# Values centred where they are stored, and a readout with its sums on VectorE and a scaling on ScalarE

## The chip, the cores and the metric

The kernel runs on one core of a Trainium2 chip. TensorE (PE in the profile) multiplies matrices, VectorE (DVE), ScalarE (ACT) and GpSimd (POOL) work elementwise, and SyncE (SP) issues most transfers. The metric is the device time of one execution in microseconds, as the median of three runs. All data are float32; a product of two float32 matrices is made of three passes over high and low halves (H and L in the names).

## The reference

Two layers over 256 context tokens and 2048 latent tokens, 1024 wide: an RWKV mixer with 16 heads of 64, and a differential attention. The change touches the mixer's scan and its readout.

```python
def step(S, inp):
    r_t, w_t, k_t, v_t, kk_t, a_t = inp
    sa = jnp.einsum("bhvk,bhk->bhv", S, kk_t)
    S = (S * w_t[:, :, None, :]
         - sa[..., None] * (kk_t * a_t)[:, :, None, :]
         + v_t[..., None] * k_t[:, :, None, :])
    return S, jnp.einsum("bhvk,bhk->bhv", S, r_t)
...
mean = jnp.mean(o, axis=-1, keepdims=True)
var = jnp.mean(jnp.square(o - mean), axis=-1, keepdims=True)
y = ((o - mean) * lax.rsqrt(var + GN_EPS)).reshape(B, T, RW_WIDTH) * gn_g + gn_b
bonus = jnp.sum(jnp.sum(r[:, :, None] * kd * r_k, axis=-1, keepdims=True) * v[:, :, None], axis=2)
y = (y + bonus.reshape(B, T, RW_WIDTH)) * jax.nn.silu(g)
return y.astype(out_dtype) @ w_out
```

The scan starts from a state of zero and is linear in v, and each of the 64 rows of a head's state depends on its own element of v alone. So the mean of o over a head's 64 values is what the scan gives for the mean of v over them, and if v is centred per head and token, o comes out centred. The bonus uses v itself.

## The kernel before, in words

The program has stages, one after another: the first projection and the streams of the scan (to about 1150 us), the scan (to about 2250 us), the readout (to about 2600 us), the second projection, attention and its output projection.

**First projection.** Three groups of tokens, and in each eight pairs of heads. For every pair PE projects its columns (`project`, L363), and DVE and ACT make the streams of the scan from them. `by_token` turns the pair's values by PE's transposes, ACT copies them into the tile `vtok` (128 partitions, 6 blocks of tokens x 2 x 2 x 64), and after every second pair two transfers on SP store them (`S["v"]`, L550). So `vtok` is full 12 times. The gate of the pair is made by ACT and by two products on DVE (`sg`, L574). The weights of the next pair are cast on ACT, and their low half is a subtraction on DVE (`wL` and `w2L`, L92). The order of each engine is set by a scheduler here.

**Readout.** There are 18 tiles of 128 tokens. A tile needs: the sum of the two directions of the scan (`of`+`ob`, L972); its mean, the subtraction and the square (L977 to L980); the variance (L983, L984); the inverse root, an integer seed (L70) and three Newton steps of three instructions on a tile `st` of 17 columns (L72, L73, L79), 16 for the heads and one for the norm below; the product with it (`ob`, L988); eight transposes on PE (L995) and two products with the gate (L996); the sum with the bonus (`sgg`+`bv`, L998); and its halves `yH` (ACT, L91) and `yL` (DVE, L92). `product` multiplies them with the output weights, 48 matmuls (L932) in four quarters. `sums` multiplies a half of the result by a gate on DVE (`gated`, L1021) and adds it to x on POOL (L1022). `norms` squares and sums x on ACT (L1029), scales the sum (L1030), multiplies x by the inverse root (L1032), transposes it on PE (L214), which ACT brings into `ht` (L220), and stores `ht` for the second projection. Seven transfers of 512 KB belong to a tile: of, ob, sgg, bv and x in, x and ht out.

These are generators: each `yield` ends a step of a tile. The string `READ` says in which order the steps are issued in one round, and `in_order` makes each engine keep this order. A is the next step of the rows of the tile two ahead, B of the tile one ahead, M0 to M3 are the four quarters of this tile's product, G is `sums` of its first half, H `sums` of the second half of the tile before, N is a step of `norms` of the tile before, R a Newton step. One root instruction serves the 16 variances of the tile two ahead and the norm of the tile before. The pools hold two tiles each of `of`, `ob`, `sgg`, `bv`, `yH`, `yL` and `ht`, and three of x. Before the first round the first two tiles are worked ahead, in between the casts of the output weights (`split`).

## Time and profile before

| what | value |
|---|---|
| median of 3 runs | 5019.62 us (5014.31 to 5025.64) |
| profiled execution | 5014.9 us, its span 5013.2 us |
| PE busy | 4677.5 us (93%) |
| DVE busy | 3764.6 us (75%) |
| ACT busy | 2678.0 us (53%) |
| POOL busy | 1510.5 us (30%) |
| mean granted PE clock | 0.967 |
| readout, 2285 to 2597 us | PE 248.96 us busy, DVE 264.44 us |

A busy share is an average over stages. The span is what the profiler recorded; the profiled execution took 1.7 us longer. PE's clock has two levels, 2.4 GHz (1.00 in the profile) and 1.2 GHz (0.50). Lines such as L932 are those of the code above; a helper's line (L70 to L79, L91, L92, L214, L220) serves several stages, and the names of the tiles tell them apart.

### The profile page before, as it was taken

How to read it: one execution, taken by the hardware profiler on the slowest of the kernel's cores; microseconds unless marked ns; L12 is line 12 of the kernel's file. 1: busy time of each engine (PE TensorE's matmuls, PEld its weight loads, DVE VectorE, ACT ScalarE, POOL GpSimd, SP SyncE). 2: the span in 40 equal slices, each digit the busy share in tenths (PEclk: the TensorE clock that was granted, in tenths of full speed). 3: DMA queues.
4: the chain of work that ended last, by engine and by line, in shares of the span. 5: the costliest groups of instructions: out<-in, count | busy, mean ns of one | idle time of the engine just before them, and what ended most of it. 6: DMA issues, size and time to landing. Idle time of an engine off the chain costs nothing.

```text
span 5013.2 us, 101038 instructions
## 1 busy us (share of the span) xinstructions
PE 4677.5 (93%) x40786; PEld 4202.4 (84%) x40786; DVE 3764.6 (75%) x5833; ACT 2678.0 (53%) x4890; POOL 1510.5 (30%) x1840
## 2 busy tenths in 40 slices
PE   6999999997988989897879999999999999999999
PEld 5999999995888888875668888878888888898887
DVE  6778777777777778758878348328989989988843
ACT  4555555554666666653342122117777777777730
POOL 1121112113665566633322022022233323323300
PEclk8999999998999999988889999999999999999999
DMA  4565566557677666676653233240111011010042
GB/s 165 165 185 165 165 184 176 164 157 208 154 172 170 167 160 170 169 228 212 202 183 106 94 125 98 88 119 1 28 45 36 11 45 36 27 28 18 9 156 93
DMA packets 624787, 612.13 MB, mean 122 GB/s; under 512 B 31622, under 2 KB 529721, under 8 KB 623297
## 3 DMA queue, kind: packets, MB, share of 16 engines
q1 hardware_dynamic: 621841, 601.99, 41.6%
q8 instruction: 323, 5.29, 0.5%
q10 hardware_dynamic: 2480, 3.67, 0.3%
q14 instruction: 143, 1.17, 0.1%
HBM read 405.79 MB, written 199.77 MB: 121 GB/s over the span
## 4 chain that ended last, share of the span: by engine, by line
PE 36%; DVE 6%; issue 5%; ACT 2%; POOL 1%; DMA 0%; POOLq 0%; ACTq 0%; DVEq 0%; SPq 0%
PE mmps L932 16%; PE pv L1451 8%; PE tps L1444 4%; PE sc L1405 3%; PE sc L1406 3%; DVE p L1408 3%; DVE p L1429 2%; PE tps L1354 1%; DVE r L1426 1%; ACT at L1446 1%; ACT p L1419 1%; POOL out L1279 0%; PE tps L1594 0%; ACT ht L220 0%; ACT qt L1385 0%
## 5 line engine op out<-in xcount | busy, mean ns | idle before, releaser
L1419 ACT ACTIVATE p<-p,m 128x2304 f32<-128x2304 f32 x256 | 568.8, 2222 | 201.0 <-DVE p L1408 198.4
L1451 PE MATMUL pv<-v,at 128*128 128x128 f32 x4608 | 626.4, 277 | 6.3 <-ACT at L1446 4.4
L1451 PEld LDWEIGHTS pv<-v,at 128*128 128x128 f32 x4608 | 564.4, 192 | 16.2 <-ACT at L1446 12.9
L1405 PE MATMUL sc<-ks,qh 128*128 128x512 f32 (+1 forms) x1280 | 520.6, 407 | 15.3 <-DVE p L1408 15.2
L1406 PE MATMUL sc<-ks,ql 128*128 128x512 f32 (+1 forms) x1280 | 464.0, 372 | 0.3 <-POOL ql L1386 0.3
L363 PE MATMUL mmps<-hH,wH 128*128 128x386 f32 x1632 | 432.1, 345 | 18.6 <-DVE sg L574 12.3
L1446 ACT COPY at<-tps 128x512 f32<-128x512 f32 (+1 forms) x640 | 345.2, 540 | 179.4 <-PE tps L1444 175.5
L1429 DVE SCALAR_TENSOR_TENSOR p<-p,r,p 128x1152 f32<-128x1152 f32 x256 | 426.9, 1668 | 4.5
L363 PE MATMUL mmps<-hL,wH 128*128 128x386 f32 x1632 | 427.8, 342 | 2.1 <-DVE hL L92 2.1
L363 PE MATMUL mmps<-hH,wL 128*128 128x386 f32 x1632 | 426.7, 342 | 1.4 <-DVE nm_ss L197 1.2
L932 PE MATMUL mmps<-wH,hH 128*128 128x512 f32 x1088 | 424.8, 390 | 3.1 <-ACT hH L91 3.1
L932 PE MATMUL mmps<-wL,hH 128*128 128x512 f32 x1088 | 424.5, 390 | 0.0
L932 PE MATMUL mmps<-wH,hL 128*128 128x512 f32 x1088 | 424.0, 390 | 0.0
L1408 DVE TENSOR_SCALAR_CACHE_REDUCE p<-sc,m 128x1280 f32<-128x1280 f32 x256 | 395.5, 1545 | 18.1 <-PE sc L1406 1.6
L1386 POOL TENSOR_TENSOR ql<-qt,qh 128x256 fp32r<-128x256 f32 x128 | 113.5, 887 | 979.8 <-ACT qt L1385 918.5
L1444 PE MATMUL tps<-ident,p 128*128 128x128 f32 x2304 | 361.6, 275 | 10.3 <-ACT qt L1385 5.4
L1408 DVE TENSOR_SCALAR_CACHE_REDUCE p<-sc 128x1024 f32<-128x1024 f32 x256 | 311.5, 1217 | 56.7 <-PE sc L1406 55.6
L1444 PEld LDWEIGHTS tps<-ident,p 128*128 128x128 f32 x2304 | 273.2, 141 | 60.8 <-ACT at L1446 11.2
L363 PEld LDWEIGHTS mmps<-hH,wH 128*128 128x128 f32 x1632 | 298.4, 191 | 24.8 <-DVE sg L574 15.8
L363 PEld LDWEIGHTS mmps<-hL,wH 128*128 128x128 f32 x1632 | 301.4, 191 | 3.3 <-DVE hL L92 3.3
L363 PEld LDWEIGHTS mmps<-hH,wL 128*128 128x128 f32 x1632 | 302.0, 191 | 2.5 <-DVE nm_ss L197 2.0
L700 POOL TENSOR_TENSOR N<-N,rank 128x30 f32<-128x30 f32 (+14 forms) x510 | 278.8, 547 | 40.0
(315 smaller groups left out, 10779.0 us busy)
## 6 DMA issues: line engine op xcount, KB each, us to landing
wr<-in_rw_in_dram SPq DMA_DIRECT2D x102, 512.0 KB
s_qr<-QR SPq DMA_DIRECT2D x48, 768.0 KB
BK<-s_bk SPq DMA_DIRECT2D x72, 512.0 KB
s_bk<-BK SPq DMA_DIRECT2D x47, 768.0 KB
wraw<-in_da_in_dram SPq DMA_DIRECT2D x64, 512.0 KB
BA<-s_bk SPq DMA_DIRECT2D x72, 256.0 KB
LA<-s_qr SPq DMA_DIRECT2D x72, 256.0 KB
BB<-s_bk SPq DMA_DIRECT2D x72, 256.0 KB
```

Of the source, the lines that this page charges most:

```text
L363: nc.tensor.matmul(a[:, :b1 - b0], wt[:, kt, :], ht[:, kt, b0:b1], start=(kt == 0 and wt is wH and ht is hH), stop=(kt == KT - 1 and last))
L700: eng.tensor_tensor(N[:, m + 1:32, 0:m], N[:, m + 1:32, 0:m], t, op=ALU.subtract)
L932: k.nc.tensor.matmul(ps, s(kt), m(kt), start=(kt == 0 and s is sH and m is mH), stop=(kt == KT - 1 and last))
L1386: nc.gpsimd.tensor_tensor(ql, qt, qh.bitcast(F32), op=ALU.subtract)
L1405: nc.tensor.matmul(s[:, b0 - g0:b1 - g0], qh[:, cs], ks, start=True, stop=False)
L1406: nc.tensor.matmul(s[:, b0 - g0:b1 - g0], ql[:, cs], ks, start=False, stop=True)
L1408: nc.vector.tensor_scalar(tiles[n][c][:, g0:g1], s[:, :g1 - g0], -1.0, m, op0=ALU.mult, op1=ALU.min, accum_out=least)
L1419: nc.scalar.activation(P, P, AF.Exp, bias=m, scale=-1.0, accum_out=z)
L1429: nc.vector.scalar_tensor_tensor(P0[:, b0:b1], P1[:, b0:b1], r, P0[:, b0:b1], op0=ALU.mult, op1=ALU.add)
L1444: nc.tensor.transpose(ps[:, c - b0:c - b0 + 128], P0[:, c:c + 128], k.ident)
L1446: (eng.copy if eng is nc.scalar else eng.tensor_copy)(at[b][:, :b1 - b0], ps[:, :b1 - b0])
L1451: nc.tensor.matmul(acc, at[b][:, c - b0:c - b0 + 128], H.v[:, c // 128], start=(c == 0), stop=(c == T - 128))
```

## The change

It has two parts. In the first projection, when `vtok` is full, DVE sums each of its 24 groups of 64 values and subtracts a 64th of the sum from them; the store of v then takes the centred values. `vm`, from which the bonus is made, stays as it is.

In the readout the mean, its scaling and the subtraction are left out. The scalings of the variance and of the norm's sum go into the squares on ACT (by 1/8 and 1/32 before squaring), and both small constants are added by one instruction on 17 columns. The sums `of`+`ob` and `sgg`+`bv` of all tiles go to DVE, as the first tile's were before. The scaling of x by the inverse root goes from DVE to ACT. The loads of a tile become a step of their own (L, for the tile three ahead), `yL` becomes a step of its own behind `yH`, and `READ` is rewritten.

```diff
@@ -535,6 +535,8 @@
                 out = nc.scalar if end else nc.sync
 
                 def by_token(vtok):
                     if p % 2 == 0:
                         vtok = up.tile([128, 6, 2, 2, 64], F32, name="vtok", bufs=1)
                     for b in range(2):
@@ -545,6 +547,11 @@
                         nc.scalar.copy(vtok[:, 3 * b:3 * b + 3, :, p % 2, :],
                                        ps[:, :384].rearrange("p (j a v) -> p j a v", a=2, v=64))
                     if p % 2 == 1:
+                        heads = vtok.rearrange("p j a q v -> p (j a q) v")
+                        total = up.tile([128, 24], F32, name="vsum")
+                        nc.vector.tensor_reduce(total, heads, axis=AX.X, op=ALU.add)
+                        nc.vector.scalar_tensor_tensor(heads, bcast(total, 2, 64), -1.0 / 64, heads,
+                                                       op0=ALU.mult, op1=ALU.add)
                         for a in range(2):
                             c0 = a * 512 + (p - 1) * 64
                             nc.sync.dma_start(out=S["v"][gs, c0:c0 + 128].rearrange("(j p) c -> p j c", p=128),
@@ -933,7 +940,7 @@
                                stop=(kt == KT - 1 and last))
 
 
-READ = "B A A H M0 M1 A G N B R R M2 R N A M3 B N N"
+READ = "H A M0 B B N A B M1 R R R B G A N L M2 N N M3"
 
 
 def readout(k):
@@ -958,7 +965,11 @@
         gates = k.gates
         wH, wL = ([wps[half].tile([128, KT, 512], F32R, name=name) for half in range(2)] for name in ("woH", "woL"))
 
-        def rows(i, first):
+        eps = small.tile([128, 17], F32, name="eps", bufs=1)
+        nc.vector.memset(eps[:, :16], 64e-5)
+        nc.vector.memset(eps[:, 16:], 1e-6)
+
+        def rows(i):
 
 
 
@@ -969,19 +980,13 @@
             bv = gp.tile([128, NPAIR, 128], F32, name="bv")
             nc.sync.dma_start(out=flat(of), in_=S["o"][0, ts])
             nc.sync.dma_start(out=flat(ob), in_=S["o"][1, ts])
-            (nc.vector if first else nc.gpsimd).tensor_tensor(of, of, ob, op=ALU.add)
             nc.sync.dma_start(out=sgg, in_=S["sgg"][:, :, ts])
             nc.sync.dma_start(out=bv, in_=S["bv"][:, :, ts])
             yield
-            mean = small.tile([128, 16], F32, name="mean")
-            nc.vector.tensor_reduce(mean, of, axis=AX.X, op=ALU.add)
-            nc.vector.tensor_scalar(mean, mean, 1.0 / 64, None, op0=ALU.mult)
-            nc.vector.tensor_tensor(of, of, bcast(mean, 2, 64), op=ALU.subtract)
-            nc.scalar.activation(ob, of, AF.Square)
-            yield
-            var = stat.s[:, :16]
-            nc.vector.tensor_reduce(var, ob, axis=AX.X, op=ALU.add)
-            nc.vector.tensor_scalar(var, var, 1.0 / 64, 64e-5, op0=ALU.mult, op1=ALU.add)
+            nc.vector.tensor_tensor(of, of, ob, op=ALU.add)
+            nc.scalar.activation(ob, of, AF.Square, scale=1.0 / 8)
+            yield
+            nc.vector.tensor_reduce(stat.s[:, :16], ob, axis=AX.X, op=ALU.add)
             yield
             rstd = stat.y[:, :16]
             yn = flat(ob).rearrange("p (b c) -> p b c", c=128)
@@ -995,10 +1000,12 @@
                     nc.tensor.transpose(ps[:, 128 * j:128 * j + 128], yn[:, 4 * half + j], k.ident)
                 nc.vector.tensor_tensor(sgg[:, hs], ps.rearrange("p (a b) -> p a b", b=128), sgg[:, hs], op=ALU.mult)
                 yield
-            (nc.vector if first else nc.gpsimd).tensor_tensor(sgg, sgg, bv, op=ALU.add)
+            nc.vector.tensor_tensor(sgg, sgg, bv, op=ALU.add)
             yH = yp.tile([128, NPAIR, 128], F32R, name="yH")
             yL = yp.tile([128, NPAIR, 128], F32R, name="yL")
-            split_evac(k, yH, yL, sgg)
+            nc.scalar.copy(yH, sgg)
+            yield
+            nc.vector.tensor_tensor(yL, sgg, yH.bitcast(F32), op=ALU.subtract)
             yield yH, yL
 
         def product(i, yH, yL):
@@ -1025,11 +1032,9 @@
 
             def norms():
                 h = hp.tile([128, KT, 128], F32, name="ht")
-                ss = stat.s[:, 16:17]
-                nc.scalar.activation(flat(h), x, AF.Square, accum_out=ss)
-                nc.vector.tensor_scalar(ss, ss, 1.0 / D, 1e-6, op0=ALU.mult, op1=ALU.add)
+                nc.scalar.activation(flat(h), x, AF.Square, scale=1.0 / 32, accum_out=stat.s[:, 16:17])
                 yield
-                nc.vector.tensor_scalar(x, x, stat.y[:, 16:17], None, op0=ALU.mult)
+                nc.scalar.activation(x, x, AF.Copy, scale=stat.y[:, 16:17])
                 yield
                 for half in range(2):
                     flip_half(k, 1, which, tpb, x, h, 0, half)
@@ -1040,7 +1045,7 @@
 
         N = T // 128
         order = (1, 0, *range(2, N))
-        todo = [rows(i, j == 0) for j, i in enumerate(order)]
+        todo = [rows(i) for i in order]
 
         raws = {}
 
@@ -1067,6 +1072,8 @@
 
         def roots(c0, c1):
 
+            s = stat.s[:, c0:c1]
+            nc.vector.tensor_tensor(s, s, eps[:, c0:c1], op=ALU.add)
             for stat.y in rsqrt_steps(k, small, stat.s, 17, "st", c0=c0, c1=c1):
                 yield
 
@@ -1089,8 +1096,9 @@
                         load_gate(k, 0, which, gates[which])
             split(0)
             split(1)
-            for _ in range(3):
+            for _ in range(4):
                 y = step(todo[0])
+            step(todo[2])
             split(2)
             split(3)
         none = iter(())
@@ -1099,6 +1107,7 @@
             for j in range(N + 1):
                 nxt = todo[j + 1] if j + 1 < N else none
                 after = todo[j + 2] if j + 2 < N else none
+                far = todo[j + 3] if j + 3 < N else none
                 stat.s = small.tile([128, 17], F32, name="stat")
                 root = roots(0 if j + 2 < N else 16, 17 if j else 16)
                 if j < N:
@@ -1110,6 +1119,8 @@
                     kind = what[0]
                     if kind == "A":
                         step(after)
+                    elif kind == "L":
+                        step(far)
                     elif kind == "B" and j + 1 < N:
                         y = step(nxt)
                     elif kind == "M":
```

How the change moves instructions is seen at three places. In a step of the readout on DVE, before: from the scaling of x to the norm's sum, between two blocks of roots (`st`, 10 instructions that are left out here).

```order
L1032 TENSOR_SCALAR x<-x,st_y 128x1024
L988 TENSOR_TENSOR ob<-of,st_y 128x2x8x64
L92 TENSOR_TENSOR yL<-sgg,yH 128x1024
L996 TENSOR_TENSOR sgg<-tps,sgg 128x512
L977 TENSOR_REDUCE mean<-of 128x16
L978 TENSOR_SCALAR mean<-mean 128x16
L979 TENSOR_TENSOR of<-of,mean 128x1024
L1021 TENSOR_TENSOR gated<-mmps,gate_27254 128x512
L983 TENSOR_REDUCE stat<-ob 128x16
L984 TENSOR_SCALAR stat<-stat 128x16
L1021 TENSOR_TENSOR gated<-mmps,gate_27254 128x512
L1030 TENSOR_SCALAR stat<-stat 128x1
```

And after, at the same place (the roots stand before the first row and behind the last):

```order
L1008 TENSOR_TENSOR yL<-sgg,yH 128x1024
L1028 TENSOR_TENSOR gated<-mmps,gate_27290 128x512
L993 TENSOR_TENSOR ob<-of,st_y 128x2x8x64
L1028 TENSOR_TENSOR gated<-mmps,gate_27290 128x512
L986 TENSOR_TENSOR of<-of,ob 128x1024
L1001 TENSOR_TENSOR sgg<-tps,sgg 128x512 x2
L989 TENSOR_REDUCE stat<-ob 128x16
L1003 TENSOR_TENSOR sgg<-sgg,bv 128x1024
L1076 TENSOR_TENSOR stat<-stat,eps 128x17
```

Between two blocks of roots stand the two sums and one reduction; both products with the gate (`sgg`<-`tps`) stand together behind `of`+`ob`, and no scaling of x is left on DVE.

On ACT, one step of the readout before and the start of the next:

```order
L91 CAST yH<-sgg 128x1024
L220 ACTIVATE ht<-tps,mod_127 128x128 x8
L980 ACTIVATE ob<-of 128x1024
L1029 ACTIVATE ht,stat<-x 128x1024
L91 CAST yH<-sgg 128x1024
```

And after:

```order
L1037 ACTIVATE x<-x,st_y 128x1024
L220 ACTIVATE ht<-tps,mod_127 128x128 x8
L987 ACTIVATE ob<-of 128x1024
L1035 ACTIVATE ht,stat<-x 128x1024
L1006 CAST yH<-sgg 128x1024
```

The scaling of x stands between yH and the eight copies into `ht`, whose transposes read it.

On DVE in the first projection, the piece of the difference around the first new pair of instructions (`wr` and `w2r` are raw weights, `sg` is the gate):

```order
 L92 TENSOR_TENSOR wL<-wr,wH 128x1024
-L574 SCALAR_TENSOR_TENSOR sg<-sg,mmps 128x386 x2
+L581 SCALAR_TENSOR_TENSOR sg<-sg,mmps 128x386 x2
+L552 TENSOR_REDUCE vsum<-vtok 128x24
+L553 SCALAR_TENSOR_TENSOR vtok<-vsum,vtok 128x1536
 L92 TENSOR_TENSOR w2L<-w2r,w2H 128x512
 L402 TENSOR_TENSOR uk<-uk,km 128x768
```

The pair stands behind the gate's products and ahead of the low half of the weights; in some of the 12 places another instruction stands between the two.

## Rows read from the trace of the kernel before

**Rows 1.** Stages (us): busy time and instructions per engine, PEclk, DMA share, GB/s.

```profile
20.00:1160.00 1140.00, 1084.71 (x6191) 1046.92 (x6188) 875.11 (x1368) 641.39 (x1077) 223.54 (x180) 0.97 0.57 170
...
2222.00:2285.00 63.00, 45.97 (x541) 35.57 (x540) 41.18 (x63) 28.29 (x41) 7.67 (x4) 0.78 0.87 289
2285.00:2597.00 312.00, 248.96 (x1072) 206.13 (x1072) 264.44 (x391) 105.08 (x200) 118.17 (x66) 0.87 0.59 186
```

**Rows 2.** PE's waits, 2285 to 2600 us: total, times, longest.

```profile
PE tps L214 <- DVE x L1032: 57.1, 17, 5.4
```

**Rows 3.** The tile yL: duration min/median/max in ns, first and last start.

```profile
L92 DVE TENSOR_TENSOR yL<-sgg,yH x18: 1216/1219/1224, 2268.8 to 2583.1; 128x1024 fp32r<-128x1024 f32 x18
```

**Rows 4.** Timeline of one step of the readout: start, duration in us, engine, line.

```profile
2426.73 0.60 PE L995 MATMUL tps<-ident,ob 128*128 128x128 f32 x4
...
2427.78 0.68 DVE L996 TENSOR_TENSOR sgg<-tps,sgg 128x512 f32<-128x512 f32 x1
...
2429.09 2.39 POOL L998 TENSOR_TENSOR sgg<-sgg,bv 128x1024 f32<-128x1024 f32 x1
2429.20 2.32 DVE L72 TENSOR_TENSOR st_t<-st_y 128x17 f32<-128x17 f32 x1
...
2431.55 0.18 DVE L73 SCALAR_TENSOR_TENSOR st_t<-st_t,stat 128x17 f32<-128x17 f32 x1
2431.77 0.18 DVE L79 SCALAR_TENSOR_TENSOR st_y<-st_t,st_y 128x17 f32<-128x17 f32 x1
...
2432.29 2.35 POOL L972 TENSOR_TENSOR of<-of,ob 128x1024 f32<-128x1024 f32 x1 [0.81 <-issue]
2432.41 2.27 DVE L79 SCALAR_TENSOR_TENSOR st_y<-st_t,st_y 128x17 f32<-128x17 f32 x1
2432.44 0.39 PE L932 MATMUL mmps<-woH,yL 128*128 128x512 f32 x1
...
2436.07 1.22 DVE L988 TENSOR_TENSOR ob<-of,st_y 128x1024 f32<-128x1024 f32 x1
2436.30 1.94 PE L214 MATMUL tps<-ident,x 128*128 128x128 f32 x8 [3.47 <-DVE x L1032]
2437.21 1.22 DVE L92 TENSOR_TENSOR yL<-sgg,yH 128x1024 fp32r<-128x1024 f32 x1
```

**Rows 5.** Groups of 2285 to 2585 us: times run, busy us, mean ns, idle before.

```profile
L72 DVE TENSOR_TENSOR st_t<-st_y 128x17 f32<-128x17 f32 x45 | 42.1, 936 | 1.6
L1022 POOL TENSOR_TENSOR x<-x,gated 128x512 f32<-128x512 f32 x32 | 41.4, 1294 | 173.9 <-DVE gated L1021 120.2 <-issue 21.9 <-DMA wraw<-in_da_in_dram 13.3
...
L979 DVE TENSOR_TENSOR of<-of,mean 128x1024 f32<-128x1024 f32 x15 | 18.4, 1225 | 0.5
...
L977 DVE TENSOR_REDUCE mean<-of 128x16 f32<-128x1024 f32 x15 | 18.1, 1209 | 0.0
...
L1029 ACT ACTIVATE ht<-x 128x1024 f32<-128x1024 f32 x16 | 17.0, 1060 | 14.3 <-POOL x L1022 13.4 <-DMA x<-in_x_dram 0.9
...
L1032 DVE TENSOR_SCALAR x<-x,st_y 128x1024 f32<-128x1024 f32 x16 | 12.1, 753 | 1.9 <-DVE st_y L79 0.4
```

**Rows 6.** Slices of 1 us: PE busy (x), PEclk, DMA share, GB/s.

```profile
2439.00:2440.00 1.00, 1.00 (x4) 0.50 0.91 373
...
2441.00:2442.00 1.00, 1.00 (x4) 0.52 0.81 203
```

**Rows 7.** The chain of waits in the last stage: start, us, what.

```profile
4877.11 0.44 PE tps L1594 x4
4877.55 10.94 PE mmps L932 x48
```

**Rows 8.** Timeline of DVE before the first round of the readout.

```profile
2234.41 1.22 DVE L972 TENSOR_TENSOR of<-of,ob 128x1024 f32<-128x1024 f32 x1 [1.95 <-DMA ob<-s_o]
```

**Rows 9.** Timeline of PE at the end of the readout.

```profile
2597.55 1.09 PE L214 MATMUL tps<-ident,x 128*128 128x128 f32 x8 [2.20 <-DVE x L1032]
```

**Rows 10.** PE's waits in the first projection, 20 to 1160 us.

```profile
PE mmps L363 <- DVE sg L574: 12.3, 11, 2.3
```

## The prediction

> **What bounds the kernel now.** The table by stages comes first [rows 1]. In the first projection (20 to 1160 us) TensorE (PE) is busy for 1084.71 of 1140 us at a granted clock of 0.97: little to gain there. The readout (2285 to 2597 us) is the weak stage: PE 248.96 of 312 us, VectorE (DVE) 264.44, a clock of 0.87. The table of PE's waits names one cause: the transposes of x (L214) wait for DVE's scaling of x (L1032), 57.1 us in 17 times [rows 2]. A step is measured by yL, which DVE writes once a tile: 18 times from 2268.8 to 2583.1 us, 17 intervals, 314.3/17 = 18.49 us each [rows 3].
>
> Why the scaling is late stands in one step [rows 4]. POOL starts sgg+bv (L998) at 2429.09 for 2.39 us; beside it a DVE instruction of 17 elements takes 2.32 us, where its neighbours take 0.18. At 2432.29 POOL starts of+ob (L972) for 2.35 us, and again a small one takes 2.27. So each POOL sum costs DVE some 2.1 us, in the middle of the roots that the scaling needs. The groups say that this is the rule: 45 root instructions of one kind average 936 ns [rows 5]. PE's last matmul ends at 2432.83, and its transposes start at 2436.30 after 3.47 us idle. The second loss follows: the granted clock is at 0.50 (1.2 instead of 2.4 GHz) when they run, for 1.94 us, and comes back only in 2441 to 2442 [rows 6].
>
> **What PE needs.** At the full clock 48 matmuls take 10.94 us, 0.228 each, and 4 transposes 0.44 [rows 7]. A step has 48 matmuls (four quarters M0 to M3 of 2.73 us) and 16 transposes (two groups of 0.87 us): 10.94+1.74 = 12.7 us. That is the floor of a step.
>
> **The change, readout.** Per tile it takes the mean (1.21) and the subtraction (1.225) off DVE, three scalings of 16 or fewer columns (I price them as the small instructions, 0.18 [rows 4]), and the scaling of x, 0.75 [rows 5]: 3.7 us. It adds of+ob and sgg+bv, and one sum of 17 elements. On DVE the sum of+ob of the first tile took 1.22 [rows 8], and sgg+bv has the same shape. So DVE pays 2.4 and is rid of two stalls of 2.1: 4.2 us. Large sums with nothing to wait for start 1.14 us apart (2436.07, 2437.21), that is 0.08 less than their length; for 512 elements (0.68) that gives 0.60; dependent small ones start 0.21 apart (I take 0.213) [rows 4].
>
> The step in the new order, from the start of M0:
> - M0 ends at 2.73. Four transposes of ob (0.60 in a row at full clock, against 0.44 in the middle of a run [rows 7]; I take 0.60) and 0.05 to DVE: 3.38.
> - DVE multiplies two halves of sgg, 1.20: 4.58. Then the variance's reduction 1.14 and sgg+bv 1.14: 6.86. The reduction needs ScalarE's (ACT) square of of+ob, which starts when DVE's sum is done, about 2.1, and takes 1.06 [rows 5].
> - 11 small instructions (the sum with eps, the seed and 9 of three root steps) by 0.213: 9.20.
> - x is scaled on ACT. No row has this form with 1024 elements; between DVE's 0.75 and ACT's square of 1024 elements, 1.06 [rows 5], I take 1.06 (its own engine) and 0.05 on either side: 10.36.
> - Eight transposes 0.87: 11.23. M3 2.73: **14.0 us**.
> PE has M1 and M2 between its two groups of transposes and ends them at 2.73+0.87+5.46 = 9.06, so it waits 1.3 us, for ACT instead of DVE. What is late next is this one wait. DVE goes on with yL, one gated product and ob until about 12.7, hence ahead of the next M0; yH and yL are done 3 us before they are needed. POOL keeps the two sums of x (1.29 each [rows 5]); one may stall DVE's of+ob by up to 1.3 us, from 0.8 to 2.1, and DVE has nothing then before 3.38, so up to 0.3 us of it is felt. All loads of a tile stand one tile earlier and in another order on SP; the load of ob can go when the transposes of the tile before last have read its buffer, 3.6 us into a step, and is needed by of+ob 0.8 us into the next, 11 us later. 7 transfers of 512 KB per step are 3.67 MB in 14 us, 262 GB/s; one slice shows 373 [rows 6].
>
> Does the clock stay up with a wait of 1.3 us? After a wait of 2.20 us in the last tile the 8 transposes took 1.09 us, near the full clock's 0.87; after 3.47 us they took 1.94 [rows 4, 9]. I take the full clock.
>
> Gain: 17 x (18.49-14.0) = 76 us. Before the first yL (2268.84) two tiles' means, scalings and subtractions leave the chain, 2 x 2.6 us [rows 5]: 5 us (0 to 10; ACT's order around it changes too). Two steps also cast the next weights on ACT and DVE, two casts of 1024 elements each, as yL 1.2 us on DVE [rows 3]: 4 us of the gain is not had. The first steps run beside the stage's densest transfers (289 GB/s [rows 1]): another 4.
>
> **The change, first projection.** After every second pair of heads DVE gets a reduction of 1536 elements and a product-and-sum over them, 12 times. The nearest rows are the reduction and the subtraction of 1024 elements, 1.21 and 1.225 [rows 5]; by length 1.75 to 1.8 each, 3.5 a pair, 42 us on DVE, which is idle for 265 of 1140 us [rows 1]. They stand behind the gate's two products (L574) and before the weights' low half (L92 w2L) and uk. PE waited for DVE's gate products 12.3 us in 11 times, its most costly wait in this stretch [rows 10]; the new pair stands behind these products, and what comes after it (the next low halves, uk) PE needs later. The store of v now waits for DVE, and behind it on SP stand loads of weights used about a head later. I take 2 us, with 0 and 42 as ends. A gain is excluded: nothing is removed here. At the end of the stage the store of v delays the scan's first loads: 2 us (0 to 4). The rest of the program is as it was; the last tile adds 0.5 us for a scaling on ACT.
>
> **Sum.** -76-5+4+4+2+2+0.5 = -68.5 us. The profiled execution took 5014.9 us (span 5013.2, 1.7 around it); so 4946 for it. The median of the runs is 5019.6, 4.7 above: **4951 us**.
>
> **Rivals.**
> - *The clock falls in every step, as now.* A wait of 1.3 us then costs as much clock as 3.47 does now: from 2436.3 to 2441.9, 5.6 us at half, 2.6 us a step. Step 16.6, gain 17 x 1.9 = 32: 4995 us; with every second step about 4973. For: the stage now shows 0.87; against: [rows 9]. 0.17.
> - *PE alone sets the step.* If the roots end 1.3 us sooner than I reckon, the step is 12.7, 17 x 5.8 = 98: 4929 us. 0.08.
> - *DVE stays the bound.* It is busy for 264.44 of 312 us and gets 2.4 us of sums per step. If its stalls of 4.2 us stayed in the chain in another shape (POOL's sums of x, late loads of ob), x would be scaled at 14.6 and the step be 18.2: 17 x 0.3 = 5 us of gain there, 5022 us. Against: only sums of 1024 elements on POOL stand beside the long small instructions [rows 4], and these go. 0.03. The Trainium skill, "Perfetto Trace Analysis", section "Optimizing Scalar/DVE Operations", speaks for this rival: from a saturated VectorE work may be handed to ScalarE or even GpSimd, and the change hands two sums the other way. The same section adds that these two share an SBUF read port, so that offloading between them might not help; with that the rows agree, a stall of 2.1 us against 1.2 us for doing the sum oneself.
> - *Transfers set the step.* 3.67 MB at the stage's 186 GB/s [rows 1] are 19.7 us, so no gain: 5015 to 5025 us. The 373 GB/s of one slice speak against it [rows 6]. 0.02.
> - *Slower: the centring lands on PE's path.* Its pair of 3.5 us stands before w2L, uk and BK on DVE, and if PE waits for them it loses 3.5, a spell at half clock as in the readout (2.6), and some of the delay of the weights' loads that stand on SP behind the late store (up to 3.5 more; I take 1): 7.1 a pair, 12 of them 85 us against 2 in the sum, 5034 us. It decides from 5.9 us a pair (70.5/12). For: PE is busy for 95% of this stage, so nothing there hides a wait. Against: DVE idles for 22 us per pair (265/12). 0.05.
> That the change does not do what it says is excluded by its code: no sum of sgg or of is left on POOL.
>
> **Chances and range.** The forecast 0.65, with 4935 to 4972 from the ends above (a step of 13.5 to 14.8, startup, phase 1 up to 12). The two ends of the range take in the floor and most of the first rival: 4929 to 4988. Faster by over 0.2% (10 us, about what a measurement can tell): 0.65+0.17+0.08 = 0.90; within (the two rivals of no gain): 0.05; slower: 0.05.
>
> **What would show it.** Right: yL at intervals near 14.0; small DVE instructions in the roots at 0.18 throughout; PE's wait at the transposes of x (L214) 1 to 2 us and named after ACT; a clock near 1.00 from the second step on; first projection within 5 us of its length. Wrong: a wait above 2 us there with transposes of 1.9 us (the clock), a wait of DVE's of+ob for its loads (transfers), a longer first projection with PE waiting for w2L or hL (the centring).

## The result and the profile after

The changed kernel takes 4959.27 us (median of 4 runs, 4953.41 to 4979.01) against 5018.75 (4 runs, 5014.31 to 5025.64): ratio 0.9885, 95% interval 0.9861 to 0.9909. On another chip, later, it took 4959.15 (6 runs) against 5028.34 (12 runs): 0.9869 (0.9843 to 0.9895). The prediction was 4951, 4929 to 4988. It holds, and is 8 us low.

The tile yL measures the step, as in [rows 3]: a step is the time from one of its starts to the next.

```profile
L1008 DVE TENSOR_TENSOR yL<-sgg,yH x18: 1217/1218/1226, 2276.0 to 2518.1; 128x1024 fp32r<-128x1024 f32 x18
```

242.1 us for 17 intervals, 14.24 each, against 18.49. From the fourth to the fifteenth all are 14.2 (14.17 on average); the first three are 16.2, 11.6 and 14.1, the last two 15.7 and 14.6. PE's waits of 2285 to 2535 us (total, times, longest) answer to [rows 2]:

```profile
PE tps L214 <- ACT x L1037: 19.5, 14, 2.8
PE tps L214 <- issue: 3.3, 2, 2.0
```

The 57.1 us behind DVE have become 19.5 behind ACT, 1.4 a time. The stage by engines, as in [rows 1] (PE, PEld, DVE, ACT, POOL, clock, DMA share, GB/s):

```profile
2285.00:2535.00 250.00, 224.75 (x1094) 183.79 (x1093) 175.54 (x353) 124.88 (x218) 72.60 (x35) 0.99 0.78 248
```

The granted clock went from 0.87 to 0.99, and DVE from 264.44 of 312 us to 175.54 of 250. The groups of that stretch answer to [rows 5]; the root instruction of 17 columns, 936 ns before, takes 178:

```profile
L1029 POOL TENSOR_TENSOR x<-x,gated 128x512 f32<-128x512 f32 x35 | 72.6, 2075 | 256.2 <-DVE gated L1028 138.3 <-ACT x L1037 106.8 <-DMA s_ht<-ht 4.9
...
L1003 DVE TENSOR_TENSOR sgg<-sgg,bv 128x1024 f32<-128x1024 f32 x17 | 20.7, 1217 | 0.0
...
L1037 ACT ACTIVATE x<-x,st_y 128x1024 f32<-128x1024 f32 x17 | 19.5, 1149 | 21.0 <-DVE st_y L79 18.3 <-DVE gated L1028 2.7
...
L72 DVE TENSOR_TENSOR st_t<-st_y 128x17 f32<-128x17 f32 x45 | 8.0, 178 | 1.6
```

One step in the timeline (start, duration, engine), to be laid beside [rows 4] and beside the prediction's list:

```profile
2403.05 1.15 ACT L1037 ACTIVATE x<-x,st_y 128x1024 f32<-128x1024 f32 x1 [1.16 <-DVE st_y L79]
2404.34 1.06 PE L214 MATMUL tps<-ident,x 128*128 128x128 f32 x8 [1.29 <-ACT x L1037]
...
2404.83 2.15 POOL L1029 TENSOR_TENSOR x<-x,gated 128x512 f32<-128x512 f32 x1 [7.75 <-ACT x L1037]
...
2408.28 0.69 DVE L1028 TENSOR_TENSOR gated<-mmps,gate 128x512 f32<-128x512 f32 x1 [2.45 <-PE mmps L939]
2408.89 1.21 DVE L986 TENSOR_TENSOR of<-of,ob 128x1024 f32<-128x1024 f32 x1
2411.37 1.29 DVE L1001 TENSOR_TENSOR sgg<-tps,sgg 128x512 f32<-128x512 f32 x2 [1.27 <-PE tps L1000]
2412.58 1.21 DVE L989 TENSOR_REDUCE stat<-ob 128x16 f32<-128x1024 f32 x1
2413.70 1.22 DVE L1003 TENSOR_TENSOR sgg<-sgg,bv 128x1024 f32<-128x1024 f32 x1
2414.83 0.17 DVE L1076 TENSOR_TENSOR stat<-stat,eps 128x17 f32<-128x17 f32 x1
...
2416.95 0.18 DVE L79 SCALAR_TENSOR_TENSOR st_y<-st_t,st_y 128x17 f32<-128x17 f32 x1
```

From the products with the gate (2411.37) to the eps sum (2414.83) are 3.46 us, to the last root instruction's end (2417.13) 5.76; the prediction had 3.48 and 5.82. PE's wait of 1.29 stands where 1.3 was forecast.

Where the 61.5 us between the two spans (5013.2, 4951.7) lie, by the starts of the named instructions in the two timelines, and in the second profile of the changed kernel:

| stretch | before | after | difference | second profile |
|---|---|---|---|---|
| start to the scan's first matmul | 1151.5 | 1154.7 | +3.2 | 1159.9 |
| scan, to the first of+ob | 1082.9 | 1094.8 | +11.9 | 1081.7 |
| to the first yL | 34.4 | 26.5 | -7.9 | 26.3 |
| 17 intervals of yL | 314.3 | 242.1 | -72.2 | 242.7 |
| last yL to the second projection's first matmul | 27.3 | 32.2 | +4.9 | 32.2 |
| the rest | 2402.8 | 2401.3 | -1.5 | 2404.4 |

### The profile page after: what moved, and what is told of

It reads as the page before. It is cut to its first block, busy times and chain, and to the rows that moved or that the text cites. A ratio compares the mean times of both kernels' runs of the same rounds, so it can differ in the third digit from the quotient of the medians.

```text
span 4951.7 us, 100950 instructions
## 1 busy us (share of the span) xinstructions
PE 4658.2 (94%) x40786; PEld 4184.8 (85%) x40786; DVE 3706.7 (75%) x5806; ACT 2700.0 (55%) x4908; POOL 1457.7 (29%) x1806
## 4 chain that ended last, share of the span: by engine, by line
PE 62%; DVE 14%; issue 11%; DMA 5%; ACT 5%; POOL 2%; SPq 0%; ACTq 0%; POOLq 0%; DVEq 0%
PE mmps L939 18%; PE mmps L363 9%; PE pv L1462 8%; PE tps L1455 4%; PE sc L1416 4%; PE sc L1417 3%; PE xops L818 3%; PE scps L680 3%; DVE p L1419 3%; PE xops L796 3%; DVE p L1440 2%; DMA RS<-s_v 2%; PE chps L813 1%; PE tps L1365 1%; DVE U L742 1%
## 5 line engine op out<-in xcount | busy, mean ns | idle before, releaser
L1462 PEld LDWEIGHTS pv<-v,at 128*128 128x128 f32 x4608 | 564.3, 191 | 16.0 <-ACT at L1457 12.8
L363 PE MATMUL mmps<-hH,wH 128*128 128x386 f32 x1632 | 429.5, 343 | 17.1 <-DVE sg L581 12.0
L1419 DVE TENSOR_SCALAR_CACHE_REDUCE p<-sc,m 128x1280 f32<-128x1280 f32 x256 | 395.5, 1545 | 17.1 <-PE sc L1417 1.2
L363 PEld LDWEIGHTS mmps<-hH,wH 128*128 128x128 f32 x1632 | 297.7, 191 | 21.1 <-DVE sg L581 15.5
```

The source lines that it names most:

```text
L363: nc.tensor.matmul(a[:, :b1 - b0], wt[:, kt, :], ht[:, kt, b0:b1], start=(kt == 0 and wt is wH and ht is hH), stop=(kt == KT - 1 and last))
L1419: nc.vector.tensor_scalar(tiles[n][c][:, g0:g1], s[:, :g1 - g0], -1.0, m, op0=ALU.mult, op1=ALU.min, accum_out=least)
L1462: nc.tensor.matmul(acc, at[b][:, c - b0:c - b0 + 128], H.v[:, c // 128], start=(c == 0), stop=(c == T - 128))
```

## Experiments

The theory after the result: a step is set by one chain, from the transposes of ob to the scaling of x, and the new order lets this chain begin early and meet no stall; centring, sums and scaling count only as far as they lie on it. The rivals: the two sums on POOL were the whole matter, or the means were. The runs vary the means, the sums, the engine of the scaling and the order. Steps are the mean of 17 intervals in the run's profile; ratios are to the kernel before on the same chip.

**1. Centring alone.** The kernel before with these lines of the change:

```diff
                     if p % 2 == 1:
+                        heads = vtok.rearrange("p j a q v -> p (j a q) v")
+                        total = up.tile([128, 24], F32, name="vsum")
+                        nc.vector.tensor_reduce(total, heads, axis=AX.X, op=ALU.add)
+                        nc.vector.scalar_tensor_tensor(heads, bcast(total, 2, 64), -1.0 / 64, heads,
+                                                       op0=ALU.mult, op1=ALU.add)
```

> The kernel before, with only the centring of v in the first projection added; the readout still takes its (now zero) means. Theory (the 24 new instructions lie in DVE's idle time, except in the last pair of heads, where they stand ahead of uk and PE waits 3.7 us longer): first matmul of the scan about 3 us later, readout steps unchanged at 18.5, time 3 to 5 us above before. Rival (centring lands on PE's path in every pair): 20 us or more above. Second rival (SP's order in the scan, which changes with the centring, costs the 12 us by which the scan of the changed kernel was longer): scan 12 us longer here as well, time 15 us above before.

Measured: 5041.63 us against 5026.09, ratio 1.0032 (1.0015 to 1.0050), so 8 to 25 us slower; steps 18.50. The first projection is not as free as the theory had it. PE's waits of 20 to 1156 us in this kernel:

```profile
PE mmps L363 <- DVE sg L579: 13.5, 11, 2.6
...
PE mmps L363 <- DVE hL L92: 8.4, 2, 4.6
PE msps L436 <- DVE uk L430: 2.7, 2, 1.3
```

and in the kernel before:

```profile
PE mmps L363 <- DVE hL L92: 2.1, 3, 0.8
...
PE msps L436 <- DVE uk L430: 1.8, 1, 1.8
```

The gate's products are awaited as before, but the low halves of the next group's input (hL) come later, 8.4 us against 2.1 in two places. The two waits for uk (from which the bonus is summed) shown for this kernel are new and come right behind those; the one at the end of the stage, 1.8 before, is 5.5 here and lies behind the stretch shown. The same 8.4 stands in the changed kernel, and 2.1 and 2.2 in runs 4 and 5, which do not centre.

The time, 15.5 us above, is not the theory's 3 to 5 but what the second rival named. In this profile, whose span is 34.9 us longer, the scan starts 8.2 us later and is 27.6 us longer. Whether the centring is the cause of the longer scan is taken up under "The scan" below.

**2. The sums back on POOL.**

```diff
-            nc.vector.tensor_tensor(of, of, ob, op=ALU.add)
+            (nc.vector if i == 1 else nc.gpsimd).tensor_tensor(of, of, ob, op=ALU.add)
...
-            nc.vector.tensor_tensor(sgg, sgg, bv, op=ALU.add)
+            (nc.vector if i == 1 else nc.gpsimd).tensor_tensor(sgg, sgg, bv, op=ALU.add)
```

> The changed kernel with both sums of 1024 elements back on POOL (DVE for the first tile). Theory (the two sums on POOL stall DVE by 2.1 us each, and taking them off POOL was the main gain): steps of yL 16 to 17 us instead of 14.24, PE's wait above 3 us, the clock falls again, time 4990 to 5010. Rival (the new order alone moves the sums to where DVE reads PSUM or waits, so that they block nothing): steps within 0.5 us of 14.24, time 4955 to 4968.

Measured: 4978.46 us, ratio 0.9902 (0.9880 to 0.9924); steps 14.70, twelve of them 14.4. The rival holds in the steps: no root instruction in them is long, since POOL's sums now stand elsewhere. The time is between the two forecasts, 10 us above the rival's and 12 below the theory's. The timeline, DVE and POOL:

```profile
2412.57 2.38 POOL L986 TENSOR_TENSOR of<-of,ob 128x1024 f32<-128x1024 f32 x1
2413.71 1.29 DVE L1001 TENSOR_TENSOR sgg<-tps,sgg 128x512 f32<-128x512 f32 x2 [2.47 <-PE tps L1000]
2415.13 2.42 POOL L1003 TENSOR_TENSOR sgg<-sgg,bv 128x1024 f32<-128x1024 f32 x1 [0.18 <-DVE sgg L1001]
2416.08 1.22 DVE L989 TENSOR_REDUCE stat<-ob 128x16 f32<-128x1024 f32 x1 [1.08 <-ACT ob L987]
2417.40 0.18 DVE L1076 TENSOR_TENSOR stat<-stat,eps 128x17 f32<-128x17 f32 x1
```

One sum of 2.38 us runs beside products that read PSUM, which keep their 1.29 for two; the other beside a reduction of 1.22. The eps sum starts 0.1 us after the reduction, behind no stall. It comes 3.69 us behind the start of the products, against 3.46 in the changed kernel: POOL needs 2.38 us for of+ob instead of 1.21, so its square is late, and the reduction waits 1.08 us for it. In this order the engine of the two sums is worth half a microsecond a step on average, 0.2 in the regular ones.

**3. The scaling of x back on DVE, in its place.**

```diff
-                nc.scalar.activation(x, x, AF.Copy, scale=stat.y[:, 16:17])
+                nc.vector.tensor_scalar(x, x, stat.y[:, 16:17], None, op0=ALU.mult)
```

> The changed kernel with the scaling of x by the inverse root back on DVE. Theory (the chain from the transposes of ob to the scaling of x sets the step, and DVE's 0.75 us without a hand-over is 0.35 shorter than ACT's 1.06): steps 13.9, time about 6 us below the changed kernel. Rival (DVE's busy time sets the step): steps 14.9, time about 11 us above it.

Measured: 5046.48 us, ratio 1.0042 (1.0023 to 1.0060): slower than the kernel before. Steps 19.00. Both expectations are wrong, because they overlooked what stands ahead of it in DVE's queue:

```profile
2399.95 1.22 DVE L1008 TENSOR_TENSOR yL<-sgg,yH 128x1024 fp32r<-128x1024 f32 x1
2401.08 0.68 DVE L1028 TENSOR_TENSOR gated<-mmps,gate 128x512 f32<-128x512 f32 x1
2401.68 1.22 DVE L993 TENSOR_TENSOR ob<-of,st_y 128x1024 f32<-128x1024 f32 x1
...
2402.82 1.75 DVE L1037 TENSOR_SCALAR x<-x,st_y 128x1024 f32<-128x1024 f32 x1
...
2404.71 1.94 PE L214 MATMUL tps<-ident,x 128*128 128x128 f32 x8 [4.59 <-DVE x L1037]
```

The roots end at 2400.03. The scaling starts 2.8 us later, takes 1.75 (POOL's sum of x runs from 2401.84 to 2404.01), and PE waits 4.59; its transposes run at half the clock.

**4. The sums on DVE in the old order.**

```diff
-            (nc.vector if first else nc.gpsimd).tensor_tensor(of, of, ob, op=ALU.add)
+            nc.vector.tensor_tensor(of, of, ob, op=ALU.add)
...
-            (nc.vector if first else nc.gpsimd).tensor_tensor(sgg, sgg, bv, op=ALU.add)
+            nc.vector.tensor_tensor(sgg, sgg, bv, op=ALU.add)
```

> The kernel before with only the two sums of all tiles on DVE: old order, means kept. Theory (the stalls by POOL were the cause, 4.2 us a step against 2.3 for doing the sums): PE's wait falls from 3.4 to about 1.5 us, the clock stays up, steps 14.2 to 16.6, time 4945 to 4990. Rival (the means and the order matter as much): PE's wait stays above 2.5 us, the clock still falls, steps above 17, time above 4995.

Measured: 5010.20 us, ratio 0.9957 (0.9943 to 0.9970); steps 17.29. The stalls are gone, as the theory said, and the granted clock is back at 0.97 from 0.87 [rows 1]. But 1.2 us a step is all that came of it: less than the 4.2 of stalls minus 2.4 for the sums, although the clock was regained as well. Steps and time fall on the rival's side, although PE waits only 1.3 us a time for x, where the rival had more than 2.5. PE's waits of 2300 to 2580 us show the new ones, and the row of 2300 to 2500 us the clock:

```profile
PE mmps L932 <- ACT yH L91: 23.2, 16, 1.5
PE tps L214 <- DVE x L1032: 17.9, 14, 5.5
PE mmps L932 <- DVE yL L92: 7.4, 14, 0.5
```

```profile
2300.00:2500.00 200.00, 163.76 (x741) 126.14 (x740) 167.56 (x295) 67.69 (x133) 29.66 (x23) 0.97 0.67 210
```

In the old order sgg+bv stands on DVE behind the scaling of x and ob, and the next M0 waits for yH and yL. While POOL made this sum beside the roots, yH was early. The scaling of x, now earlier, also waits in 11 steps (9.1 us in all) until x has been stored, since it overwrites x.

**5. The means kept in the new order.** The changed kernel without the lines of run 1, and with

```diff
             nc.vector.tensor_tensor(of, of, ob, op=ALU.add)
+            mean = small.tile([128, 16], F32, name="mean")
+            nc.vector.tensor_reduce(mean, of, axis=AX.X, op=ALU.add)
+            nc.vector.tensor_scalar(mean, mean, 1.0 / 64, None, op0=ALU.mult)
+            nc.vector.tensor_tensor(of, of, bcast(mean, 2, 64), op=ALU.subtract)
```

> The changed kernel without the centring of v, and with the mean, its scaling and the subtraction (2.5 us on DVE) put back behind the sum of+ob, in the new order. Theory (DVE idles there for 1.3 us until the transposes of ob are done, so half of the 2.5 us is hidden and the rest lengthens the chain to the scaling of x): steps 15.4 to 15.7 if the clock holds at a wait of 2.6 us, 17 to 18 if it falls; the first projection's end 3 us earlier. Rival (centring is worth nothing beside the order): steps 14.3.

Measured: 4998.40 us, ratio 0.9949 (0.9930 to 0.9967); steps 16.67, most of them 17.1. So the second branch: PE's wait is about 2.7 us and the clock falls. PE's waits of 2295 to 2540 us, and the stage's row of 2300 to 2540 us, clock 0.90:

```profile
PE tps L214 <- ACT x L1036: 34.8, 13, 3.0
```

```profile
2300.00:2540.00 240.00, 200.91 (x890) 165.19 (x890) 177.53 (x322) 102.17 (x184) 61.31 (x29) 0.90 0.67 214
```

So 1.3 us more of waiting cost 2.4 to 2.9 us a step. The rest is the clock: in a regular step PE is busy for 14.3 us here (200.91 of 240, of 17.1) and for 12.8 in the changed kernel (224.75 of 250, of 14.2), with the same work.

**6. The scaling on DVE, directly behind the roots.** Run 3 with another place for N, measured on two chips:

```diff
-READ = "H A M0 B B N A B M1 R R R B G A N L M2 N N M3"
+READ = "H A M0 B B N A B M1 R R R N B G A L M2 N N M3"
```

> The changed kernel with the scaling of x on DVE, as in the run before, but issued directly behind the roots: N stands ahead of the B of yL, so ahead of yL, a gated product and the product ob. Theory (it was the place behind these three that cost 4.8 us a step, 3.0 us of DVE's work, a stall and the clock; the engine itself matters little): steps 13.7 to 14.2. Rival (a scaling on DVE is slow wherever it stands, because POOL's sum of x stalls it): steps above 16.

> The scaling of x on DVE directly behind the roots, once more, beside the changed kernel. Theory: steps 13.8, 0.4 us shorter, so 5 to 8 us less in the readout and in the time. Rival: the step is regained elsewhere, time equal.

Measured: 4953.67 us, ratio 0.9873 (0.9844 to 0.9902), steps 13.82; and 4954.27, 0.9861 (0.9834 to 0.9889), steps 13.86. Place, not engine, made the 4.8 us of run 3. Behind the roots DVE is 0.4 us a step quicker than ACT. Beside the changed kernel's 4959.15 the time alone does not tell the two apart; the steps do (13.8 against 14.2, all from the third on).

**7. The old order without means.** Run 1 with these lines taken out:

```diff
-            mean = small.tile([128, 16], F32, name="mean")
-            nc.vector.tensor_reduce(mean, of, axis=AX.X, op=ALU.add)
-            nc.vector.tensor_scalar(mean, mean, 1.0 / 64, None, op0=ALU.mult)
-            nc.vector.tensor_tensor(of, of, bcast(mean, 2, 64), op=ALU.subtract)
```

> The kernel before with the centring and without the mean, its scaling and the subtraction; old order, sums on POOL. Theory (in the old order DVE's whole step lies on the chain to the scaling of x, and the two stalls stay): 2.5 us less per step, PE's wait 3.4 becomes about 1, steps 14 to 16. Rival (the stalls by POOL only move, and the sum of+ob on POOL, 2.4 us, is now awaited by the square): steps 17 or more.

Measured: 5021.85 us against 5027.11, ratio 0.9995 (0.9979 to 1.0011); steps 18.20. The rival holds, though by another way than it says:

```profile
2421.04 0.24 DVE L985 TENSOR_SCALAR stat<-stat 128x16 f32<-128x16 f32 x1
2425.68 0.69 DVE L1022 TENSOR_TENSOR gated<-mmps,gate 128x512 f32<-128x512 f32 x1 [4.39 <-PE mmps L937]
...
2427.86 2.31 DVE L72 TENSOR_TENSOR st_t<-st_y 128x17 f32<-128x17 f32 x1
2430.20 2.36 DVE L73 SCALAR_TENSOR_TENSOR st_t<-st_t,stat 128x17 f32<-128x17 f32 x1
```

In the old order G (the gated product of M1) stands ahead of the roots. The 2.5 us taken off DVE ahead of it turn into waiting for M1: 4.39 us in this step, 40.0 in 14 steps of 2300 to 2580 us, against 11.2 in 9 in the kernel before. Both stalls still stand behind it, now one after the other.

**8. The chain cut.** The changed kernel with

```diff
-READ = "H A M0 B B N A B M1 R R R B G A N L M2 N N M3"
+READ = "H A M0 B B N A M1 R R R N B G A B L M2 N N M3"
...
-                    if p % 2 == 1:
+                    if p % 2 == 1 and not end:
+                        centre(vtok)
+                    return vtok
+
+                def centre(vtok):
+                    if True:
...
                     next(pending)
                     next(pending)
+                    centre(vtok)
```

> The changed kernel with two more moves. In READ, sgg+bv goes from ahead of the roots to behind them, the scaling of x directly behind the roots on ACT, and yL to the end of DVE's step (H A M0 B B N A M1 R R R N B G A B L M2 N N M3). And in the last pair of heads the centring is issued behind the bonus. Theory (the chain to the scaling of x is 1.14 us shorter, PE's wait of 1.3 all but goes and PE's own 12.7 us set the step): steps 12.9, time 20 to 24 us below the changed kernel's, PE's wait for uk at the end of the first projection 2 us shorter. Rival (yH, behind the scaling of x on ACT, and yL come too late for the next M0): steps 14 or more, PE waiting for yH or yL.

Measured: 4970.06 us, ratio 0.9903 (0.9873 to 0.9933), while the changed kernel has 0.9885 and 0.9869: the 20 us below it that the theory forecast did not come. The steps are uneven: 18.1 and 14.8 at first, then 13.2 to 13.8 with one of 14.3 and one of 15.5, and 16.8 and 14.6 at the end; mean 14.24, as in the changed kernel. Theory and rival each hold in part. The steps of 13.2 show the shorter chain, but yL, issued behind ob, meets POOL's sum of x:

```profile
2406.99 2.15 POOL L1034 TENSOR_TENSOR x<-x,gated 128x512 f32<-128x512 f32 x1 [6.81 <-ACT x L1042]
2407.91 2.32 DVE L1013 TENSOR_TENSOR yL<-sgg,yH 128x1024 fp32r<-128x1024 f32 x1
```

The wait for uk at the end of the first projection fell from 5.5 to 3.3 us; the scan's first matmul was at 1163.9 all the same, so nothing of that is seen in the time.

**9. The changed kernel again.** No edit.

> The changed kernel once more, beside the runs below on one chip. Steps of 14.2 as before; the stages ahead of the readout may differ by 10 to 20 us from the first profile of it, if their length is a matter of the execution and not of the change.

Measured: 4959.15 us; steps 14.27. The scan took 1081.7 us, 13 less than in its first profile and 1 less than in the kernel before.

**10. PE-bound.** Run 3's scaling on DVE, and

```diff
-READ = "H A M0 B B N A B M1 R R R B G A N L M2 N N M3"
+READ = "H A M0 B B N A M1 R R R N B A B G L M2 N N M3"
```

> Scaling of x on DVE behind the roots, sgg+bv behind it, then ob, yL and the gated product (H A M0 B B N A M1 R R R N B A B G L M2 N N M3). Theory (the chain is now shorter than PE's two quarters, and yL does not stand beside POOL's sum of x as in the run with the chain cut): steps 12.7 to 13.2, time 17 to 25 us below the changed kernel's. Rival (yL comes after the next M0 is due, or the sum of x comes late for its square): steps 13.8 or more, PE waiting for yL, or DVE for the square of x.

Measured: 4946.37 us (5 runs, 4940.14 to 4952.53), ratio 0.9841 (0.9815 to 0.9867); steps 13.54, eleven of them 12.8 to 13.1. It is the fastest of all, 13 us below the changed kernel on the same chip (4948.77 to 4970.04). The theory holds for most steps; the first (17.5), two of 14.5 and 16.2 and a few of 13.3 to 13.6 keep the time from the 17 us it forecast at least. PE's waits of 2300 to 2500 us:

```profile
PE tps L214 <- DVE x L1037: 6.3, 5, 3.4
PE mmps L939 <- ACT yH L1006: 3.3, 1, 3.3
```

In most steps the scaling of x is no longer awaited. PE's 12.7 is reached to within 0.2 in ten of them.

**11. All but the order.** Run 7 with the edit of run 4 added.

> Old order, with the centring, no means, and both sums on DVE; the scaling of x stays on DVE. So all of the change except the order, the split of yL, the loads and ACT's scaling. Theory (in the old order the roots stand behind the gated product of M1, which DVE waits for, so that work taken from DVE ahead of it turns into waiting): steps 15.5 to 17, PE waiting for x or yH. Rival (the stalls were the whole matter, and without them the old order is as good): steps 14.0 to 14.5.

Measured: 4986.09 us, ratio 0.9921 (0.9893 to 0.9949); steps 16.19, some 14.9 and some 16.5. Taken singly in the old order, the sums gave 1.2 us and the means 0.3; together 2.3. DVE's waits of 2285 to 2560 us:

```profile
DVE gated L1022 <- PE mmps L937: 33.7, 15, 5.9
DVE yL L92 <- ACT yH L91: 19.0, 17, 1.2
```

DVE has time now, and spends it waiting for M1 ahead of the roots; PE waits for yH (18.9 us in 16 times). The remaining 1.95 us to 14.24 are the new order, with the split of yL, the earlier loads, ACT's scaling and the constants moved into its squares. These were not tried one by one. But ACT's scaling is not needed for the gain (13.82 in run 6, with the scaling on DVE), and DVE waits here for a load of of or ob only once, 1.6 us.

| step, us | old order | new order |
|---|---|---|
| as it was before / as changed | 18.49 | 14.24 |
| sums on DVE, means kept | 17.29 | 16.67 |
| sums on POOL, no means | 18.20 | 14.70 |
| sums on DVE, no means | 16.19 | 14.24 |

Order and means are worth most together: with the means gone, order gives 1.95 to 3.5, with the means kept 0.6; in the old order the means alone give 0.3.

## Why the prediction was right

- **The step.** Forecast 14.0, measured 14.2 in the regular ones. The chain's terms stood: 3.48 and 5.82 against 3.46 and 5.76. ACT's scaling took 1.149, not 1.06. The stalls by POOL's large sums are gone; POOL's sums of x reach DVE's of+ob no more than was allowed (1.21 to 1.23 us, once 1.70); it is POOL that is held up, as told below.
- **What the step's gain was put down to.** The prediction priced sums, means and scaling as terms, and let the order enter through the chain. Runs 4, 7 and 11 show that in the old order sums and means are worth 2.3 us of 4.25 (the scaling on ACT was not tried there); the reason given for the gain was right for the new order only.
- **The clock.** It stays at 0.99 with waits of 1.3 us, as read from [rows 4, 9]. The first rival (it falls in every step) is what run 5 does in most steps at waits of about 2.7.
- **Startup, odd steps and tail.** From the first yL to the second projection's first matmul the sum had -76 and +8, with +0.5 for the tail: -67.5. Measured -72.2+4.9 = -67.3. That the two agree to 0.2 is luck, for the single terms moved: a regular step is 0.2 longer, which takes 3 us from the gain; the odd steps (the first three and the last two) cost 1 us and not 8; and the tail 4.9, since yL now stands earlier in a step. Before the first yL -7.9 against -5 (0 to -10). This is the means: the stretch is 34.4 to 35.2 us in the four profiles that keep them and 25.8 to 27.0 in the ten that do not.
- **The step that failed: "what comes after it (the next low halves, uk) PE needs later".** The sum had 2 us for the first projection and 2 for the start of the scan. In ten profiles with the centring in its place the scan's first matmul comes at 1154.7 to 1164.0, 1159.1 on average; in the three without at 1151.5, 1152.1 and 1153.5. That is 6.7 us. PE waits 6.3 us longer for hL in two places, some 3 for uk behind them and 3.7 longer for uk at the end, since both stand on DVE behind the new pair; not all of this reaches the end of the stage. In the first profile of the changed kernel the scan starts only 3.2 us later, near the 4 of the sum. The prices of the pair itself, 1.75 each, were right (groups of 20 to 1160 us in the changed kernel):

```profile
L553 DVE SCALAR_TENSOR_TENSOR vtok<-vsum,vtok 128x1536 f32<-128x1536 f32 x12 | 21.0, 1752 | 0.2
L552 DVE TENSOR_REDUCE vsum<-vtok 128x24 f32<-128x1536 f32 x12 | 20.9, 1742 | 0.0
```

- **The scan.** Its +11.9 was in no term. Run 9 (1081.7) and run 4 (1103.5, with a program that is the same up to the readout as the kernel before) show that it varies by execution. Whether the centring costs it a few microseconds besides stays open: with it the mean is 1098.8 (ten profiles, 1081.7 to 1119.0), without it 1093.8 (three, 1082.9 to 1103.5). The medians do not settle it either: run 1 is 15.5 us above the kernel before, where the stretches outside the scan make 7 in its profile; run 9 is 69.2 below, where they make 65.
- **The rivals.** That DVE stays the bound by its busy time did not come: DVE is busy 70% of the stage. Neither did a bound by transfers, which ran at 248 GB/s. The Trainium skill's sentence, "Perfetto Trace Analysis", section "Optimizing Scalar/DVE Operations", that offloading between VectorE and GpSimd might not help, agrees with run 2: DVE is relieved of 2.4 us a step by POOL, and the step is 0.5 longer. The shared read port, which the section gives as the reason, is not what shows there: the DVE instructions beside POOL's sums keep their time, and POOL's longer sum makes the chain longer. Whether its advice to hand work from a saturated VectorE to ScalarE pays depends here on the place in VectorE's queue: run 3 is 4.8 us worse than ACT, run 6 is 0.4 better.

## What to carry to other kernels

When engines work through fixed queues, find the chain that ends in the longest wait and ask of every instruction whether it stands ahead of that chain in some queue; work removed elsewhere turns into waiting (run 7), and the same instruction three places later cost 5 us a step (runs 3 and 6). Before counting a new instruction as hidden by idle time, look at what is queued behind it at the ends of groups, where the cover is thin. A stage's regular interval in one profile tells differences of 0.4 us that total times with a spread of 20 us do not.

## What the runs showed of the hardware

- DVE and POOL instructions that both work on SBUF held each other up, in both directions: the sum of x on POOL takes 1294 ns on average before [rows 5] and 2075 after, where DVE runs large instructions beside it; DVE's yL took 2.32 us instead of 1.22 in run 8, and in run 10, beside the same sums of 512 elements, DVE's of+ob took 1.90 on average. So it is not only POOL's sums of 1024 elements that do this. Not all were held up: beside POOL's sums in run 2, the products with an operand in PSUM (tps, which PE writes) and the reduction of 1024 elements kept their time.
- The scan's length varies from 1082 to 1119 us between profiles, with the granted clock of the stretch. Run 9 (1160 to 2240 us, clock 0.95) and run 7 (1157 to 2275 us, clock 0.92):

```profile
1160.00:2240.00 1080.00, 958.73 (x18809) 867.97 (x18809) 824.07 (x1174) 670.93 (x1573) 599.45 (x1082) 0.95 0.69 175
```

```profile
1157.00:2275.00 1118.00, 992.76 (x18843) 901.88 (x18844) 823.65 (x1172) 671.23 (x1574) 592.72 (x1080) 0.92 0.66 169
```

  What makes the clock differ there was not tried.
- With the same two short waits of PE in every step, the clock of run 11 fell in some steps and stayed in others. PE was busy for 2.34 of the 4 us from 2408 (1.60 and 0.74), and the clock stayed at 1.00. It was busy for 2.34 of the 4 us from 2424 as well (0.87 and 1.47), and at 2428 the clock was at 0.50. What makes the difference was not tried.

```profile
2408.00:2410.00 2.00, 1.60 (x14) 1.00 0.24 47
2410.00:2412.00 2.00, 0.74 (x3) 1.00 0.74 255
...
2424.00:2426.00 2.00, 0.87 (x7) 1.00 0.77 252
2426.00:2428.00 2.00, 1.47 (x7) 0.96 0.66 175
2428.00:2430.00 2.00, 2.00 (x6) 0.50 1.05 373
```

- ACT's scaling of 128x1024 by a value per partition took 1149 ns, its square of the same tile 1060.
